# Queries, keys and values stored tile by tile, queries in half-tile buffers: a hybrid attention block on one core

## The chip, the cores and the metric

The kernel runs on one core of a Trainium2 chip. The metric is the device time of one execution in microseconds (us). A core has five engines that run side by side, each with its own in-order list of instructions: TensorE (PE, matrix products), VectorE (DVE), ScalarE (ACT), GpSimd (POOL) and SyncE (SP), which here issues every DMA. Sixteen DMA engines move data between DRAM and the on-chip memory of 128 partitions.

## The reference

One decoder block over 2048 tokens of width 1024, in float32:

```python
h = rmsnorm(x, norm1_g)
p = h @ w_in                                  # 2560 columns: pool 256, diff q/k/v 512 each, sb q/k/v 256 each
a = pool_mixer(p[pool])                       # trailing means over 2/4/8/16 tokens, 64x64 maps
b = (softmax(q1 k1') - lam * softmax(q2 k2')) v   # 4 differential heads, causal, two 64-wide maps, 128-wide values
c = A v                                       # 4 stick-breaking heads of 64, A[t,s] = sigmoid(z_ts) * prod (1 - sigmoid(z_tj))
x = x + concat(a, norm(b), norm(c)) @ w_out
x = x + (silu(h2 @ w_gate) * (h2 @ w_up)) @ w_down,  h2 = rmsnorm(x, norm2_g)
return rmsnorm(x, final_norm_g)
```

## The kernel before

The work has three parts, all of them planned together: `a1_tile` (L534) normalizes a tile of 512 tokens and projects it with the ten 256-column units of W_in; `attention` (L838) goes over the query tiles `t` = 0 to 3 and, in each, over six head pairs (four differential, two stick-breaking) in the order of `ORDER[t]`; `out_proj` (L936) and `mlp` (L963) follow. Almost every matrix product is made of three products of a high and a low part (`mm3`, L473), so queries, keys and values are stored as high and low parts too. They go to DRAM from `a1_tile` and come back in `attention`.

Nothing is issued in the order of the source. Each operation is handed to a planner (`Plan`, L102) with its engine, an estimated duration in ns, what it reads and writes, and a priority; `schedule` (L145) plays the operations against these estimates and fixes the order of every engine, and `issue` emits them in that order. All DMAs form one list, issued by SP. A buffer comes from a `Ring` (L70) of slots; a slot that two rings share passes to the second one when the first has made its last buffer. Projections of later tiles have low priority on TensorE and fill what attention leaves.

The parts that the change touches:

- DRAM layout (L301 to L304): `q_d[p]` and `k_d[p]` hold, for a pair, the high and the low part of all 2048 tokens in 128 rows (two 64-wide maps or heads); `vd_d[p]` and `vs_d[h]` hold the values.
- Stores (L586 to L613): the values of a block of 256 tokens go out per head (L595). Queries are scaled by 0.125 and split by ScalarE (L601) and VectorE (L603), keys by `split` (L414), and each goes out as one store of 512 KB (L611).
- `load_q` (L622) takes a buffer from ring `q0` for the high parts and one from `q1` for the low parts, and fills each with two loads, since the 64 rows are wanted twice, in partitions 0 to 63 and 64 to 127. Ring `q0` owns slots 31 and 12, `q1` slots 32 and 13 (L1399); 12 and 13 first belong to ring `wr` (L1386), the raw weights of `a1_tile`.
- `load_kv` (L632) loads one chunk of 512 keys: two loads for the keys (high parts in partitions 0 to 63, low parts in 64 to 127, both maps side by side), one for the values of a differential pair (L640), two for those of a stick-breaking pair (L645).
- `scores` (L651) makes the scores of 128 queries (`g` = 0 to 3 in the tile) with a chunk: the product of the keys with the high parts (L657), that with the low parts (L658), and on the diagonal the mask (L660). A differential pair goes through `g` in order with both maps of each; a stick-breaking pair goes through all four `g` for its first head and then for its second.

Of the kernel before, what the change touches and what calls it, by code (L numbers as in the profile page):

```python
# [19 lines left out]
P = 128  # L20
# [27 lines left out]
def f32(ap):  # L48
    return ap.bitcast(F32)
# [205 lines left out]
def dve_ns(n):  # L255
    return 1.042 * n + 68
# [14 lines left out]
def dma_ns(nbytes):  # L271
    return max(nbytes / 360.0, 450.0)
# [3 lines left out]
def hybrid_block_kernel(  # L276
# [21 lines left out]
    const = ctx.enter_context(tc.tile_pool(name="const", bufs=1))  # L298
    dram = ctx.enter_context(tc.tile_pool(name="dram", bufs=1, space=bass.MemoryType.DRAM))

    q_d = [dram.tile([2, P, S], F32, name=f"q_d{p}") for p in range(PAIRS)]  # L301
    k_d = [dram.tile([2, P, S], F32, name=f"k_d{p}") for p in range(PAIRS)]
    vd_d = [dram.tile([P, S // P, 2, P], F32, name=f"vd_d{p}") for p in range(DIFF_PAIRS)]
    vs_d = [dram.tile([P, S // P, 2, 64], F32, name=f"vs_d{p}") for p in range(2 * SB_PAIRS)]  # L304
    o_d = [dram.tile([KB, P, TQ], F32, name=f"o_d{t}") for t in range(NT)]
    wo_d = [dram.tile([2, P, KB, 256], F32, name=f"wo_d{u}") for u in range(4)]
    x2_d = [dram.tile([4, P, D], F32, name=f"x2_d{t}") for t in range(NT)]
# [226 lines left out]
    def a1_tile(pl, rg, t, prio, prio_pe, first):  # L534
# [8 lines left out]
            pl.op("dma", 450, lambda: nc.sync.dma_start(g1_sb, g1), w=[c_g1], prio=prio_x)  # L543
        hk = norm_transpose(pl, rg, first if t == 0 else rg["dense"], rg["hk"], xs, g1_sb, c_g1, prio_x, prio_pe, t == 0)
        if t == 0:
            constants(pl, {"w": rb["q1"], "h": rb["p0"]}, prio + 0.5, xs[3:])
        late = []
        for un in UNITS[t]:
            parts = load_split(pl, rg, w_in[un], prio, xs if t == 0 and un == UNITS[0][0] else ())
# [29 lines left out]
            for c, ps in enumerate(pend):  # L579
                if un == 0:  # L580
                    late = pend
                    break
                st = rg["st"].new()
                if is_v:
                    nh, e = (2, 128) if un != 9 else (4, 64)
                    stv = lambda st=st, nh=nh: st.t.rearrange("p a (h b l e) -> p (a h) b l e", h=nh // 2, b=2, l=2)  # L586
                    pv = lambda ps=ps, nh=nh: ps.t.rearrange("p (b h e) -> p b h e", b=2, h=nh)
                    for h in range(nh):
                        split(pl, lambda h=h, stv=stv: stv()[:, h, :, 0, :], lambda h=h, stv=stv: stv()[:, h, :, 1, :],
                              lambda h=h, pv=pv: pv()[:, :, h, :], TQ // nh, True, [ps], (st, (h, 0)), (st, (h, 1)),  # L590
                              prio)
                        dst = vs_d[h] if un == 9 else vd_d[2 * (un - 5) + h]
                        pr = DIFF_PAIRS + h // 2 if un == 9 else 2 * (un - 5) + h
                        blk0 = 4 * t + 2 * c
                        pl.op("dma", dma_ns(P * 4096 // nh), lambda dst=dst, blk0=blk0, h=h, stv=stv: nc.sync.dma_start(  # L595
                            dst[:, blk0:blk0 + 2, :, :], f32(stv()[:, h])), r=[(st, (h, 0)), (st, (h, 1))],
                            w=[(m_v[pr][t], (c, h))], prio=prio)
                else:
                    isq = un in (1, 2, 7)
                    if isq:  # L600
                        pl.op("act", act_ns(TQ), lambda st=st, ps=ps: nc.scalar.mul(st.t[:, 0, :], ps.t, 0.125),  # L601
                              r=[ps], w=[(st, 0)], prio=prio)
                        pl.op("dve", dve_ns(TQ), lambda st=st, ps=ps: nc.vector.scalar_tensor_tensor(  # L603
                            st.t[:, 1, :], ps.t, 0.125, f32(st.t[:, 0, :]), ALU.mult, ALU.subtract),
                            r=[ps, (st, 0)], w=[(st, 1)], prio=prio)
                    else:
                        split(pl, lambda st=st: st.t[:, 0, :], lambda st=st: st.t[:, 1, :], lambda ps=ps: ps.t,
                              TQ, True, [ps], (st, 0), (st, 1), prio)
                    pair = {1: 0, 2: 2, 7: 4, 3: 0, 4: 2, 8: 4}[un] + c
                    dst, mk = (q_d, m_q) if isq else (k_d, m_k)  # L610
                    pl.op("dma", dma_ns(P * 4096), lambda st=st, dst=dst[pair]: nc.sync.dma_start(  # L611
                        dst[:, :, t0:t0 + TQ].rearrange("l p t -> p l t"), f32(st.t)),
                        r=[st], w=[mk[pair][t]], prio=prio)  # L613
        for c, ps in enumerate(late):
            pool_mix(pl, rg, t, c, ps, prio, prio_pe)
        for hf, (wh, wl) in enumerate(load_split(pl, rg, w_out[t], prio)):
# [3 lines left out]


    def load_q(pl, rg, t, p, prio):  # L622
        q = [rg["q0"].new(), rg["q1"].new()]
        for hl in range(2):
            for dup in range(2):
                pl.op("dma", dma_ns(64 * 4096) * 1.3, lambda hl=hl, dup=dup: nc.sync.dma_start(
                    f32(q[hl].t[64 * dup:64 * dup + 64]),
                    q_d[p][hl, :, t * TQ:(t + 1) * TQ].rearrange("(r d) t -> d r t", r=2)),
                    r=[m_q[p][t]], w=[(q[hl], dup)], prio=prio)
        return q  # L630

    def load_kv(pl, rg, p, j, prio):  # L632
        k, v = rg["k"].new(), rg["v"].new()
        for hl in range(2):
            pl.op("dma", dma_ns(64 * 4096) * 1.3, lambda hl=hl: nc.sync.dma_start(
                f32(k.t[64 * hl:64 * hl + 64]),
                k_d[p][hl, :, j * TQ:(j + 1) * TQ].rearrange("(r d) t -> d r t", r=2)),
                r=[m_k[p][j]], w=[(k, hl)], prio=prio)
        if p < DIFF_PAIRS:
            pl.op("dma", dma_ns(P * 4096), lambda: nc.sync.dma_start(  # L640
                f32(v.t), vd_d[p][:, 4 * j:4 * j + 4].rearrange("p b l e -> p (b l e)")),
                r=[m_v[p][j]], w=[v], prio=prio)
        else:
            for r in range(2):
                pl.op("dma", dma_ns(P * 2048), lambda r=r: nc.sync.dma_start(  # L645
                    f32(v.t[:, r * TQ:(r + 1) * TQ]),
                    vs_d[2 * (p - DIFF_PAIRS) + r][:, 4 * j:4 * j + 4].rearrange("p b l e -> p (b l e)")),
                    r=[m_v[p][j]], w=[(v, r)], prio=prio)
        return k, v

    def scores(pl, rg, q, kt, r, g, j, t, strict, prio):  # L651
        n = TQ if j < t else (g + 1) * P
        s = rg["s"].new()
        qs = slice(g * P, (g + 1) * P)

        def qk():
            nc.tensor.matmul(s.t[:, :n], q[0].t[:, r, qs], kt.t[:, r, :n], start=True, stop=False)  # L657
            nc.tensor.matmul(s.t[:, :n], q[1].t[:, r, qs], kt.t[:, r, :n], start=False, stop=j < t)  # L658
            if j == t:
                nc.tensor.matmul(s.t[:, n - P:n], identb, masks[:, strict, :], start=False, stop=True)  # L660

        pl.op("pe", 2 * mm_ns(n) + (60 if j == t else 0), qk, r=[*q, kt], w=[s], prio=prio)
        return s, n

    def weighted(pl, rg, rows, nkp, pv, q0, vmm, v_bufs, nmm, prio):
# [710 lines left out]
    def banks(ids):  # L1376
# [19 lines left out]
    )  # L1396
    rb.update(
        k=ring([2, TQ], F32R, ("w", R(23, 27)), ("w", R(0, 2))), v=ring([D], F32R, ("w", R(27, 31)), ("w", R(2, 4))),
        q0=ring([2, TQ], F32R, ("w", [31, 12])), q1=ring([2, TQ], F32R, ("w", [32, 13])),  # L1399
        p0=ring([TQ], F32, ("h", R(7, 15)), ("w", [20, 21])), p1=ring([TQ], F32, ("h", R(15, 20))),  # L1400
        th=ring([TQ], F32R, ("h", [20, 21, 22, 4])), tl=ring([TQ], F32R, ("h", [23, 24, 25, 5])),
        w=ring([TQ], F32, ("h", R(26, 28))), iv=ring([TQ + 1], F32, ("h", R(28, 30))),
# [70 lines left out]
```

## Time and profile before

| | |
|---|---|
| median of 3 runs | 2723.2 us (2714.47 to 2727.28) |
| profiled execution, its own time | 2719.03 us |
| its span | 2717.2 us |
| mean granted TensorE clock | 0.977 of full speed |
| busy: TensorE, VectorE, ScalarE, GpSimd | 96%, 66%, 49%, 32% |
| DMA, mean rate | 167 GB/s, 454.27 MB |

The profile shows one execution. "PE L657 <- DMA d<-q_d" reads: TensorE's instruction of line 657 waited for a transfer from `q_d` into an on-chip buffer (all of those are called `d`). PEld is the loading of the stationary matrix, which overlaps PE; SPq is SP's list of DMA issues. A granted clock of 1.00 is 2.4 GHz; the other level is 1.2 GHz, and a stretch shows the mean. The attention part runs from about 137 us, overlapped by projections until some 900 us and by the output projection after that.

### The profile page before, as it was taken

The numbers are of one execution on the slowest core, as the hardware profiler recorded it, in microseconds if no ns is written. First come the engines' busy times: TensorE is split into PE (matmuls) and PEld (weight loads), VectorE is DVE, ScalarE is ACT, GpSimd is POOL, SyncE is SP. The second block draws the span as 40 slices with busy tenths as digits, with TensorE's granted clock in tenths as the row PEclk, the third lists the DMA queues.
The fourth block names the chain that finished last, engine by engine and source line by source line (L and its number), as shares of the span: only waits on it lengthen the run. The fifth ranks groups of instructions, "written<-read, shape, count | busy, mean of one in ns | idle before, by whom it ended". The sixth has DMA issues, their size and how long they took to land.

```text
span 2717.2 us, 39503 instructions
## 1 busy us (share of the span) xinstructions
PE 2601.9 (96%) x13836; PEld 2176.7 (80%) x13836; DVE 1786.2 (66%) x3131; ACT 1319.3 (49%) x2645; POOL 870.0 (32%) x890
## 2 busy tenths in 40 slices
PE   9989989989999999999989999999999998999998
PEld 7878778877888788888978877888888886888886
DVE  6366787758887888788656666545444447558557
ACT  4365566646666666665534444323333333445444
POOL 1001212212254124133015456535454544132041
PEclk9989999989999999999999999999999999999999
DMA  6786585556564775664534457465222338335223
GB/s 217 245 251 184 160 245 160 155 155 202 153 177 147 225 203 147 192 178 161 166 118 155 155 184 239 158 220 199 101 102 97 109 129 291 118 95 194 93 90 120
DMA packets 223480, 454.27 MB, mean 167 GB/s; under 512 B 23720, under 2 KB 70952, under 8 KB 223280
## 3 DMA queue, kind: packets, MB, share of 16 engines
q1 hardware_dynamic: 223280, 451.75, 52.9%
q8 instruction: 108, 1.77, 0.3%
q14 instruction: 92, 0.75, 0.1%
HBM read 321.11 MB, written 130.55 MB: 166 GB/s over the span
## 4 chain that ended last, share of the span: by engine, by line
PE 72%; DMA 9%; DVE 9%; issue 3%; ACT 2%; POOL 1%; SPq 1%; DVEq 0%; ACTq 0%; POOLq 0%
PE bank L474 16%; PE bank L476 16%; PE bank L475 16%; DVE d L416 4%; DMA d<-q_d 4%; PE bank L657 3%; PE bank L681 3%; PE bank L658 3%; DMA d<-wo_d 2%; PE bank L924 2%; PE bank L923 2%; PE bank L925 2%; ACT d L415 1%; PE bank L562 1%; PE bank L781 1%
## 5 line engine op out<-in xcount | busy, mean ns | idle before, releaser
L474 PE MATMUL bank<-d 128*128 128x512 f32 x2296 | 919.0, 400 | 14.0 <-DVE d L1122 9.8
L476 PE MATMUL bank<-d 128*128 128x512 f32 x2296 | 910.3, 396 | 5.7 <-DVE d L416 5.4
L416 DVE TENSOR_TENSOR d<-d 128x512 fp32r<-128x512 f32 (+2 forms) x672 | 614.6, 938 | 457.5 <-ACT d L415 281.2
L475 PE MATMUL bank<-d 128*128 128x512 f32 x2296 | 909.3, 396 | 3.4 <-DVE d L416 3.4
L415 ACT CAST d<-d 128x512 fp32r<-128x512 f32 (+2 forms) x672 | 489.0, 758 | 651.0 <-PE bank L476 352.3
L961 POOL TENSOR_TENSOR d<-d 128x512 f32<-128x512 f32 x336 | 520.0, 1556 | 846.3 <-DVE d L416 622.9
L474 PEld LDWEIGHTS bank<-d 128*128 128x128 f32 x2296 | 435.7, 190 | 116.0 <-DVE d L1122 12.4
L476 PEld LDWEIGHTS bank<-d 128*128 128x128 f32 x2296 | 434.3, 189 | 110.3 <-DVE d L416 8.7
L475 PEld LDWEIGHTS bank<-d 128*128 128x128 f32 x2296 | 434.8, 189 | 101.3 <-DVE d L416 5.1
L416 DVE TENSOR_TENSOR d<-bank,d 128x512 fp32r<-128x512 f32 (+3 forms) x381 | 219.3, 603 | 139.7 <-ACT d L415 138.7
L819 POOL TENSOR_TENSOR d<-d 128x512 f32<-128x512 f32 (+3 forms) x160 | 160.4, 1003 | 397.9 <-DVE d L815 375.6
L415 ACT CAST d<-bank 128x512 fp32r<-128x512 f32 (+3 forms) x381 | 187.5, 529 | 194.0 <-PE bank L681 122.0
L729 ACT ACTIVATE d<-bank,d 128x512 f32<-128x512 f32 (+3 forms) x320 | 198.9, 627 | 128.4 <-DVE d L726 120.3
L751 POOL TENSOR_SCALAR d<-d 128x512 f32<-128x512 f32 (+3 forms) x144 | 95.8, 681 | 448.7 <-ACT d L741 318.1
L726 DVE TENSOR_REDUCE d<-bank 128x1 f32<-128x512 f32 (+3 forms) x320 | 186.9, 602 | 61.6 <-PE bank L658 31.1
L657 PE MATMUL bank<-d 128*128 128x512 f32 (+3 forms) x480 | 203.7, 425 | 24.8 <-ACT d L729 9.0
L658 PE MATMUL bank<-d 128*128 128x512 f32 (+3 forms) x480 | 181.9, 382 | 25.5 <-DMA d<-q_d 25.5
L1122 DVE TENSOR_TENSOR d<-bank,d 128x512 f32<-128x512 f32 x176 | 121.0, 687 | 116.0 <-PE bank L476 98.7
L815 DVE TENSOR_TENSOR_SCAN d<-d,bank 128x512 f32<-128x512 f32 (+3 forms) x160 | 174.3, 1090 | 19.6 <-ACT d L807 8.1
L1118 ACT COPY d<-bank 128x512 f32<-128x512 f32 x132 | 77.3, 586 | 221.7 <-PE bank L476 196.9
L681 PE MATMUL bank<-ident,d 128*128 128x128 f32 x1088 | 157.5, 279 | 3.4 <-DVE d L772 2.6
L923 PE MATMUL bank<-d 128*128 128x256 f32 x512 | 149.5, 292 | 2.8 <-DMA d<-wo_d 1.1
(133 smaller groups left out, 3593.5 us busy)
## 6 DMA issues: line engine op xcount, KB each, us to landing
d<-in_w_gu_dram SPq DMA_DIRECT2D x88, 512.0 KB, 3.5
d<-in_w_in_dram SPq DMA_DIRECT2D x80, 512.0 KB, 4.6
d<-k_d SPq DMA_DIRECT2D x120, 256.0 KB, 6.6
d<-wo_d SPq DMA_DIRECT2D x52, 512.0 KB, 6.0
d<-q_d SPq DMA_DIRECT2D x96, 256.0 KB, 6.3
d<-vd_d SPq DMA_DIRECT2D x40, 512.0 KB, 4.9
g_d<-d SPq DMA_DIRECT2D x66, 256.0 KB, 2.1
d<-g_d SPq DMA_DIRECT2D x66, 256.0 KB, 2.7
```

Source lines behind the costliest of these rows:

```text
L415: pl.op("act", act_ns(n, psum), lambda: nc.scalar.copy(hi(), src()), r=r, w=[whi], prio=prio)
L416: pl.op("dve", dve_ns(n), lambda: nc.vector.tensor_sub(lo(), src(), f32(hi())), r=[*r, *after, whi], w=[wlo], prio=prio)
L474: nc.tensor.matmul(o, a_hi, b_hi, start=first, stop=False, **kw)
L475: nc.tensor.matmul(o, a_hi, b_lo, start=False, stop=False, **kw)
L476: nc.tensor.matmul(o, a_lo, b_hi, start=False, stop=last, **kw)
L657: nc.tensor.matmul(s.t[:, :n], q[0].t[:, r, qs], kt.t[:, r, :n], start=True, stop=False)
L658: nc.tensor.matmul(s.t[:, :n], q[1].t[:, r, qs], kt.t[:, r, :n], start=False, stop=j < t)
L681: nc.tensor.transpose(tp.t[:, c:c + P], rows[qb][kb // 4].t[:, (kb % 4) * P:(kb % 4 + 1) * P], ident)
L726: pl.op("dve", dve_ns(n), lambda s=s, n=n, mc=mc, sm=sm: nc.vector.tensor_reduce(sm.t[:, mc:mc + 1], s.t[:, :n], AX, ALU.max, negate=True) ...
L729: pl.op("act", act_ns(n, True, 2), lambda s=s, n=n, e=e, mc=mc, lc=lc, sm=sm: nc.scalar.activation(e.t[:, :n], s.t[:, :n], AF.Exp, bias=sm ...
L923: nc.tensor.matmul(o, m[:, 0, cs], wh.t[:, k % 4, :], start=k == 0, stop=False)
L961: pl.op(eng, ns, lambda: en.tensor_tensor(out(), a(), b(), op), r=r, w=w, prio=prio)
```

## The change

- In DRAM, each pair and token tile has an array of its own: `q_d[p][t]` is [2 halves of 256 queries, 64 rows, 2 maps, 2 parts (high, low), 256 queries], `k_d[p][t]` is [2 parts, 64 rows, 2 maps, 512 keys], `v_d[p][t]` is 128 rows of 1024 values.
- A query or key store becomes two stores of 64 partitions each, one for a map (or head); the query buffer that is stored now has its columns ordered half, part, query. A value store has the same size as before.
- `load_q` takes two buffers from one ring `q` with the four slots 31, 32, 12 and 13. A buffer holds one half of the tile's queries, both maps, high and low parts, and is filled by one load whose source is read twice (`to_broadcast`, leading dimension 2), for partitions 0 to 63 and 64 to 127.
- A key chunk and a value chunk are one load of 512 KB each.
- `scores` reads the buffer of its half only, and depends on that alone.
- The constants of the head take their scratch buffer from ring `q` instead of `q1`.

```diff
@@ -298,10 +298,10 @@
     const = ctx.enter_context(tc.tile_pool(name="const", bufs=1))
     dram = ctx.enter_context(tc.tile_pool(name="dram", bufs=1, space=bass.MemoryType.DRAM))
 
-    q_d = [dram.tile([2, P, S], F32, name=f"q_d{p}") for p in range(PAIRS)]
-    k_d = [dram.tile([2, P, S], F32, name=f"k_d{p}") for p in range(PAIRS)]
-    vd_d = [dram.tile([P, S // P, 2, P], F32, name=f"vd_d{p}") for p in range(DIFF_PAIRS)]
-    vs_d = [dram.tile([P, S // P, 2, 64], F32, name=f"vs_d{p}") for p in range(2 * SB_PAIRS)]
+
+    q_d = [[dram.tile([2, 64, 2, 2, 256], F32, name=f"q_d{p}_{t}") for t in range(NT)] for p in range(PAIRS)]
+    k_d = [[dram.tile([2, 64, 2, TQ], F32, name=f"k_d{p}_{t}") for t in range(NT)] for p in range(PAIRS)]
+    v_d = [[dram.tile([P, D], F32, name=f"v_d{p}_{t}") for t in range(NT)] for p in range(PAIRS)]
     o_d = [dram.tile([KB, P, TQ], F32, name=f"o_d{t}") for t in range(NT)]
     wo_d = [dram.tile([2, P, KB, 256], F32, name=f"wo_d{u}") for u in range(4)]
     x2_d = [dram.tile([4, P, D], F32, name=f"x2_d{t}") for t in range(NT)]
@@ -543,7 +543,7 @@
             pl.op("dma", 450, lambda: nc.sync.dma_start(g1_sb, g1), w=[c_g1], prio=prio_x)
         hk = norm_transpose(pl, rg, first if t == 0 else rg["dense"], rg["hk"], xs, g1_sb, c_g1, prio_x, prio_pe, t == 0)
         if t == 0:
-            constants(pl, {"w": rb["q1"], "h": rb["p0"]}, prio + 0.5, xs[3:])
+            constants(pl, {"w": rb["q"], "h": rb["p0"]}, prio + 0.5, xs[3:])
         late = []
         for un in UNITS[t]:
             parts = load_split(pl, rg, w_in[un], prio, xs if t == 0 and un == UNITS[0][0] else ())
@@ -589,28 +589,30 @@
                         split(pl, lambda h=h, stv=stv: stv()[:, h, :, 0, :], lambda h=h, stv=stv: stv()[:, h, :, 1, :],
                               lambda h=h, pv=pv: pv()[:, :, h, :], TQ // nh, True, [ps], (st, (h, 0)), (st, (h, 1)),
                               prio)
-                        dst = vs_d[h] if un == 9 else vd_d[2 * (un - 5) + h]
                         pr = DIFF_PAIRS + h // 2 if un == 9 else 2 * (un - 5) + h
-                        blk0 = 4 * t + 2 * c
-                        pl.op("dma", dma_ns(P * 4096 // nh), lambda dst=dst, blk0=blk0, h=h, stv=stv: nc.sync.dma_start(
-                            dst[:, blk0:blk0 + 2, :, :], f32(stv()[:, h])), r=[(st, (h, 0)), (st, (h, 1))],
-                            w=[(m_v[pr][t], (c, h))], prio=prio)
+                        o0, w = (h % 2 * TQ if un == 9 else 0) + 4 * c * e, 4 * e
+                        pl.op("dma", dma_ns(P * 4096 // nh), lambda dst=v_d[pr][t], o0=o0, w=w, h=h, stv=stv: nc.sync.dma_start(
+                            dst[:, o0:o0 + w], f32(stv()[:, h].rearrange("p b l e -> p (b l e)"))),
+                            r=[(st, (h, 0)), (st, (h, 1))], w=[(m_v[pr][t], (c, h))], prio=prio)
                 else:
                     isq = un in (1, 2, 7)
                     if isq:
-                        pl.op("act", act_ns(TQ), lambda st=st, ps=ps: nc.scalar.mul(st.t[:, 0, :], ps.t, 0.125),
+                        part = lambda l, st=st: st.t.rearrange("p h (l t) -> p h l t", l=2)[:, :, l, :]
+                        src = lambda ps=ps: ps.t.rearrange("p (h t) -> p h t", h=2)
+                        pl.op("act", act_ns(TQ), lambda part=part, src=src: nc.scalar.mul(part(0), src(), 0.125),
                               r=[ps], w=[(st, 0)], prio=prio)
-                        pl.op("dve", dve_ns(TQ), lambda st=st, ps=ps: nc.vector.scalar_tensor_tensor(
-                            st.t[:, 1, :], ps.t, 0.125, f32(st.t[:, 0, :]), ALU.mult, ALU.subtract),
+                        pl.op("dve", dve_ns(TQ), lambda part=part, src=src: nc.vector.scalar_tensor_tensor(
+                            part(1), src(), 0.125, f32(part(0)), ALU.mult, ALU.subtract),
                             r=[ps, (st, 0)], w=[(st, 1)], prio=prio)
                     else:
                         split(pl, lambda st=st: st.t[:, 0, :], lambda st=st: st.t[:, 1, :], lambda ps=ps: ps.t,
                               TQ, True, [ps], (st, 0), (st, 1), prio)
                     pair = {1: 0, 2: 2, 7: 4, 3: 0, 4: 2, 8: 4}[un] + c
                     dst, mk = (q_d, m_q) if isq else (k_d, m_k)
-                    pl.op("dma", dma_ns(P * 4096), lambda st=st, dst=dst[pair]: nc.sync.dma_start(
-                        dst[:, :, t0:t0 + TQ].rearrange("l p t -> p l t"), f32(st.t)),
-                        r=[st], w=[mk[pair][t]], prio=prio)
+                    for r in range(2):
+                        pl.op("dma", dma_ns(P * 2048), lambda st=st, dst=dst[pair][t], r=r, isq=isq: nc.sync.dma_start(
+                            dst[:, :, r].rearrange("h d l t -> d h (l t)" if isq else "l d t -> d l t"),
+                            f32(st.t[64 * r:64 * r + 64])), r=[st], w=[(mk[pair][t], r)], prio=prio)
         for c, ps in enumerate(late):
             pool_mix(pl, rg, t, c, ps, prio, prio_pe)
         for hf, (wh, wl) in enumerate(load_split(pl, rg, w_out[t], prio)):
@@ -620,46 +622,35 @@
 
 
     def load_q(pl, rg, t, p, prio):
-        q = [rg["q0"].new(), rg["q1"].new()]
-        for hl in range(2):
-            for dup in range(2):
-                pl.op("dma", dma_ns(64 * 4096) * 1.3, lambda hl=hl, dup=dup: nc.sync.dma_start(
-                    f32(q[hl].t[64 * dup:64 * dup + 64]),
-                    q_d[p][hl, :, t * TQ:(t + 1) * TQ].rearrange("(r d) t -> d r t", r=2)),
-                    r=[m_q[p][t]], w=[(q[hl], dup)], prio=prio)
+
+        q = []
+        for h in range(2):
+            qh = rg["q"].new()
+            q.append(qh)
+            pl.op("dma", dma_ns(P * 4096), lambda h=h, qh=qh: nc.sync.dma_start(
+                f32(qh.t), q_d[p][t][h].rearrange("(o d) r l t -> o d (r l t)", o=1).to_broadcast([2, 64, D])),
+                r=[m_q[p][t]], w=[qh], prio=prio)
         return q
 
     def load_kv(pl, rg, p, j, prio):
         k, v = rg["k"].new(), rg["v"].new()
-        for hl in range(2):
-            pl.op("dma", dma_ns(64 * 4096) * 1.3, lambda hl=hl: nc.sync.dma_start(
-                f32(k.t[64 * hl:64 * hl + 64]),
-                k_d[p][hl, :, j * TQ:(j + 1) * TQ].rearrange("(r d) t -> d r t", r=2)),
-                r=[m_k[p][j]], w=[(k, hl)], prio=prio)
-        if p < DIFF_PAIRS:
-            pl.op("dma", dma_ns(P * 4096), lambda: nc.sync.dma_start(
-                f32(v.t), vd_d[p][:, 4 * j:4 * j + 4].rearrange("p b l e -> p (b l e)")),
-                r=[m_v[p][j]], w=[v], prio=prio)
-        else:
-            for r in range(2):
-                pl.op("dma", dma_ns(P * 2048), lambda r=r: nc.sync.dma_start(
-                    f32(v.t[:, r * TQ:(r + 1) * TQ]),
-                    vs_d[2 * (p - DIFF_PAIRS) + r][:, 4 * j:4 * j + 4].rearrange("p b l e -> p (b l e)")),
-                    r=[m_v[p][j]], w=[(v, r)], prio=prio)
+        pl.op("dma", dma_ns(P * 4096), lambda: nc.sync.dma_start(
+            f32(k.t), k_d[p][j].rearrange("l d r t -> (l d) r t")), r=[m_k[p][j]], w=[k], prio=prio)
+        pl.op("dma", dma_ns(P * 4096), lambda: nc.sync.dma_start(f32(v.t), v_d[p][j]), r=[m_v[p][j]], w=[v], prio=prio)
         return k, v
 
     def scores(pl, rg, q, kt, r, g, j, t, strict, prio):
         n = TQ if j < t else (g + 1) * P
         s = rg["s"].new()
-        qs = slice(g * P, (g + 1) * P)
+        qh, c0 = q[g // 2], 2 * r * 256 + g % 2 * P
 
         def qk():
-            nc.tensor.matmul(s.t[:, :n], q[0].t[:, r, qs], kt.t[:, r, :n], start=True, stop=False)
-            nc.tensor.matmul(s.t[:, :n], q[1].t[:, r, qs], kt.t[:, r, :n], start=False, stop=j < t)
+            nc.tensor.matmul(s.t[:, :n], qh.t[:, c0:c0 + P], kt.t[:, r, :n], start=True, stop=False)
+            nc.tensor.matmul(s.t[:, :n], qh.t[:, c0 + 256:c0 + 256 + P], kt.t[:, r, :n], start=False, stop=j < t)
             if j == t:
                 nc.tensor.matmul(s.t[:, n - P:n], identb, masks[:, strict, :], start=False, stop=True)
 
-        pl.op("pe", 2 * mm_ns(n) + (60 if j == t else 0), qk, r=[*q, kt], w=[s], prio=prio)
+        pl.op("pe", 2 * mm_ns(n) + (60 if j == t else 0), qk, r=[qh, kt], w=[s], prio=prio)
         return s, n
 
     def weighted(pl, rg, rows, nkp, pv, q0, vmm, v_bufs, nmm, prio):
@@ -1396,7 +1387,7 @@
     )
     rb.update(
         k=ring([2, TQ], F32R, ("w", R(23, 27)), ("w", R(0, 2))), v=ring([D], F32R, ("w", R(27, 31)), ("w", R(2, 4))),
-        q0=ring([2, TQ], F32R, ("w", [31, 12])), q1=ring([2, TQ], F32R, ("w", [32, 13])),
+        q=ring([D], F32R, ("w", [31, 32, 12, 13])),
         p0=ring([TQ], F32, ("h", R(7, 15)), ("w", [20, 21])), p1=ring([TQ], F32, ("h", R(15, 20))),
         th=ring([TQ], F32R, ("h", [20, 21, 22, 4])), tl=ring([TQ], F32R, ("h", [23, 24, 25, 5])),
         w=ring([TQ], F32, ("h", R(26, 28))), iv=ring([TQ + 1], F32, ("h", R(28, 30))),
```

## Rows read from the trace of the kernel before

**Rows 1.** The page: the span, and busy time of each engine.

```profile
span 2717.2 us, 39503 instructions
PE 2601.9 (96%) x13836; PEld 2176.7 (80%) x13836; DVE 1786.2 (66%) x3131; ACT 1319.3 (49%) x2645; POOL 870.0 (32%) x890
```

**Rows 2.** The page: the chain that ended last, shares of the span by line.

```profile
PE bank L474 16%; PE bank L476 16%; PE bank L475 16%; DVE d L416 4%; DMA d<-q_d 4%; PE bank L657 3%; PE bank L681 3%; PE bank L658 3%; DMA d<-wo_d 2%; PE bank L924 2%; PE bank L923 2%; PE bank L925 2%; ACT d L415 1%; PE bank L562 1%; PE bank L781 1%
```

**Rows 3.** The chain in order of time: start us, us, what; query loads alone.

```profile
173.27 5.71 DMA d<-q_d
...
878.08 7.62 DMA d<-q_d
```

**Rows 4.** Waits of TensorE, 137 to 1200 us: us in total, times, longest us.

```profile
PE bank L658 <- DMA d<-q_d: 25.5, 14, 3.7
...
PE bank L657 <- DMA d<-k_d: 6.5, 3, 3.4
...
PE bank L657 <- DMA d<-q_d: 2.0, 3, 1.3
```

**Rows 5.** Timeline, 378 to 402 us: start us, us, engine, line, op, tiles, count, [idle before].

```profile
379.09 0.40 PE L658 MATMUL bank<-d 128*128 128x512 f32 x1
379.28 2.54 SPq L626 DMA_DIRECT2D d<-q_d  x4
...
387.61 0.19 PEld L658 LDWEIGHTS bank<-d 128*128 128x128 f32 x1 [1.25 <-DMA d<-q_d]
```

**Rows 6.** L657 alone by stretch: PE and PEld busy us (count), clock, DMA share, GB/s.

```profile
137.00:264.00 127.00, 18.53 (x48) 9.83 (x47) 0.93 0.73 215
...
884.00:1300.00 416.00, 83.02 (x192) 37.19 (x192) 0.97 0.62 182
```

**Rows 7.** All instructions, same stretches: busy PE, PEld, DVE, ACT, POOL, clock, DMA share, GB/s.

```profile
137.00:264.00 127.00, 115.93 (x789) 102.65 (x789) 87.82 (x202) 77.13 (x183) 14.41 (x31) 0.93 0.73 215
264.00:518.00 254.00, 235.48 (x1418) 202.74 (x1416) 192.52 (x396) 157.82 (x366) 64.49 (x108) 0.95 0.64 183
518.00:884.00 366.00, 340.96 (x1993) 289.40 (x1993) 274.16 (x494) 221.92 (x506) 112.08 (x166) 0.96 0.57 167
884.00:1300.00 416.00, 400.48 (x2740) 353.23 (x2741) 345.76 (x631) 263.16 (x612) 115.83 (x191) 0.97 0.62 182
```

**Rows 8.** DMA issues: tiles, op, count, KB each, median us from issue to landing.

```profile
d<-k_d SPq DMA_DIRECT2D x120, 256.0 KB, 6.6
...
d<-q_d SPq DMA_DIRECT2D x96, 256.0 KB, 6.3
d<-vd_d SPq DMA_DIRECT2D x40, 512.0 KB, 4.9
...
q_d<-d SPq DMA_DIRECT2D x24, 512.0 KB, 3.4
...
d<-vs_d SPq DMA_DIRECT2D x40, 256.0 KB, 4.1
...
d<-in_hsel_dram SPq DMA_DIRECT2D x1, 24.0 KB
```

**Rows 9.** Rate of the DMA engines: two stretches as in rows 7; the page's queue line.

```profile
4.00:7.00 3.00, 3.00 (x12) 1.24 (x11) 1.14 (x8) 2.30 (x4) 0.00 (x0) 1.00 0.99 393
1800.00:1850.00 50.00, 50.00 (x218) 40.54 (x217) 22.74 (x23) 15.86 (x22) 24.38 (x18) 1.00 0.95 342
q1 hardware_dynamic: 223280, 451.75, 52.9%
```

**Rows 10.** Timeline of SP around a pair boundary in tile 2.

```profile
690.93 2.96 SPq L626 DMA_DIRECT2D d<-q_d  x4
...
697.62 1.88 SPq L635 DMA_DIRECT2D d<-k_d  x3
```

**Rows 11.** SP's issues by line: count, ns min/median/max, first and last start us.

```profile
L626 SPq DMA_DIRECT2D d<-q_d x96: 573/580/1285, 38.3 to 1149.7; - x96
L611 SPq DMA_DIRECT2D q_d<-d x24: 370/374/547, 29.9 to 869.4; - x24
```

## The prediction

> **What bounds the kernel now.** I read the page first: TensorE is busy for 2601.9 us of a span of 2717.2 us [rows 1], so time is to be won or lost only where TensorE waits or where something else sets its pace. Next I read the chain of work that ended last: query loads hold 4% of it, about 100 us, the largest share of any transfer [rows 2]. In order of time these are 14 long pieces, from 173 to 878 us, of 5.7 to 8.6 us each, of which the first and the last stand here [rows 3]. A chain share is not a prize: while such a load was under way TensorE did projections that the planner had put there. What it really stood still for is in the view of waits: 25.5 us in 14 waits ahead of L658 and 2.0 us in 3 ahead of L657, together 27.5 us; key loads cost 6.5 us more [rows 4]. The timeline of one boundary between two head pairs shows why: the last score of a pair is made at 379.1 us, the four query loads of the next pair are issued at 379.3 us, as the buffer comes free, and the second product of the new pair stands until 387.6 us [rows 5]. Attention is thus single-buffered in its queries until W_in's buffers (slots 12, 13) come free. Last I cut the span where the query tiles begin: the four stretches hold 48 scores in the first to 192 in the last, 8 for each pair and chunk [rows 6], and in these TensorE's granted clock is 0.93 to 0.97, and the DMA engines are busy for 0.57 to 0.73 of the time [rows 7].
>
> **The change part by part**, against the profiled execution's own 2719.0 us (span 2717.2 and 1.8 around it); the median of the runs shown, 2723.2, is 4.2 us above it.
>
> *Buffers.* Today a pair needs two buffers until its last score; after the change each buffer holds one query half, high and low parts together, and is free when that half's scores are done. With two slots, the first half of the next pair is loaded while the second half's scores run. For differential pairs that is half a pair ahead; for a stick-breaking pair, where each half is used again for the second head, about a quarter. In tile 1 a pair lasts 254/6 = 42 us [rows 7], so 10 to 20 us stand against a landing of 6.3 us [rows 8]. If the new load lands as the old one did, all 27.5 us go: **-27.5 us**. Next late would be the key chunk.
>
> *The query load itself.* Four transfers of 256 KB become two of 512 KB, and the bytes remain the same. But the source is now a pattern whose leading dimension counts 2 (a stride of zero, to write both copies at once), where each of today's loads leads with 64 rows. The trace of before has no such load, so I bound it. From below: a 512 KB value load with 4 KB rows, 4.9 us to landing [rows 8]. From above: only as many engines carry it as the leading dimension counts, two, with 256 KB each. An engine moves 393/(0.99 x 16) = 24.8 GB/s in a stretch of wide input rows, 342/(0.95 x 16) = 22.5 in one of weight loads, and 451.75 MB/(0.529 x 16 x 2717 us) = 19.6 over the whole run [rows 9]: 10.6, 11.7 or 13.4 us a load. The nearest row is that of hsel, the one group with a leading count under 16 (8 rows): it alone, of all, has no landing time [rows 8], although its data were used. Its landing signals do not add up as those of a 64- or 128-row load do. That is a hint, not a rate, but it points to fewer engines, and I take **two engines, 11 us a load**, keeping both ends.
>
> The Trainium skill states this as a rule (DMA: Bandwidth & Descriptors, section Rules for kernel authors): an outermost dimension under 16, such as a leading broadcast without stride, confines the whole transfer to at most that many engines. By that rule the sum goes as I forecast; by the 4.9 us row alone it would be the first rival below. The hsel row agrees with it, and no run here shows its rate.
>
> What two slow engines do: every later transfer also has a sixteenth of its bytes on these two, behind the queries in one queue (SP issues all), and lands only when that part has landed. Their work by tile, from the busy shares [rows 7]:
> Tile 0, 127 us: 0.73 x 127 = 92.7 us, less 24 old loads of 16 KB an engine at 215/(0.73 x 16) = 18.4 GB/s, 21.4 us, plus 6 pairs x 2 x 11 = 132: 203 us. **+76 us**.
> Tile 1, 254 us: 162.6 - 22.0 + 132 = 273 us. **+18 us**.
> Tile 2, 366 us: 208.6 - 21.5 + 132 = 319 us, 87% full. Tile 3 with the output projection, 416 us: 257.9 - 17.9 (20 loads) + 5 x 22 = 350 us, 84%.
> In the last two the work fits, but each pair's keys can stand behind a query half: at 690.9 us the query loads go out, and three key transfers follow them at 697.6 us [rows 10]. A key load then lands up to 11 us later than now, at the price of nothing if TensorE has other work in its order and of 11 if not; I take the middle, 5.5 us for 12 pairs: **+66 us**.
>
> *Clock.* The first three tiles lost 0.07 x 127 + 0.05 x 254 + 0.04 x 366 = 36 us of clock beside 127 + 254 + 366 - 115.9 - 235.5 - 341.0 = 55 us of idle [rows 7], 0.66 us for one. About 132 us more idle could cost 87 more. I take nothing, as the stalls grow longer rather than more numerous; 87 is kept as an upper end.
>
> *Stores.* 48 stores of 512 KB become 96 of 64 partitions: 48 x 0.37 = 18 us more of SP's time; the loads save 48 + 60 + 20 issues at 0.58 us, 74 us [rows 8, 11]. SP waits for data most of the time, so neither is on the path; if SP became the limit, the net would be a gain. Runs in DRAM stay 2 KB (1 KB for stick-breaking values), so a store's landing stays near its 3.4 us [rows 8]; the store stands ahead of its reader by tens of us, except for a pair that is used as soon as its unit is done.
>
> *Keys and values.* Key loads go from two halves in 2 KB runs to 4 KB rows, stick-breaking values from two to one. At 24.8 instead of 18.4 GB/s a chunk's 32 KB an engine take 1.3 instead of 1.8 us; that is 3 to 6 us in tiles 0 and 1, taken as nothing, and with the 6.5 us of key waits a lower end of -12.
>
> *Scaling and new order.* ScalarE's and VectorE's query splits keep their element counts; only the views differ: nothing, since neither engine bounds the stage. A score now needs one half alone, so the planner lays out another order. It plans a query load at 1.5 us plus lags and knows nothing of engines; 30 us either way, about the size of the 27.5 us of waits its present error allows.
>
> Sum: 2719.0 - 27.5 + 76 + 18 + 66 = 2851.5; with 4.2 for the median, **2856 us**.
>
> **The rivals.** *Sixteen engines after all* (faster). The load lands in about 5 us, well inside half a pair; 27.5 us go, and a third of the 36 us of clock, 12: 2723 - 39 = 2684, or 2696 without the clock. For it: equal bytes, wide rows. Against it: the leading 2 and the hsel row. It decides from the point where a load's landing is below the time between a half's last score and the next pair's first, some 10 us in tile 0 (six pairs in 127 us make 21 a pair).
> *A key wait takes the place* (no change). Queries are early on sixteen engines, but the key chunk, issued when the last scores free its buffer [rows 10] and landing in 6.6 us [rows 8] against 6.3 for the queries, now holds the pair's start; 27.5 us come back as key waits: 2723. Against it: today's key waits are only 6.5 us [rows 4], and the first chunk of tiles 0 to 2 has a spare slot.
> *Two engines, but only the queries late.* If what follows is not held up, tile 0 alone pays, six pairs at about 5 us beyond the gap: 2723 - 27.5 + 30 = 2726 at the least; each bit of hold-up then moves it toward the forecast. I count this as the low edge of the forecast case.
>
> **How the numbers follow.** Two engines 0.82, sixteen engines and faster 0.12, key waits in place 0.06. About 0.5%, 14 us, is what a measurement of this kernel tells from no change; the forecast case lies beyond that but for its low edge. Its low end: 10.6 us a load, no hold-up in tiles 2 and 3, -12 for keys, -30 for order: 2719 - 27.5 + 71 + 13 - 12 - 30 + 4 = 2738. Its high end: 13.4 us a load (105 + 47 in tiles 0 and 1), 12 x 13.4 = 161, and 87 of clock: 3096. The range is cut where this case thins out, 2740 to 3070; it leaves out the rivals and little else.
>
> **What would show it.** Query loads, 48 of 512 KB, without a landing time, as hsel has none; key, value and W_in loads landing some 5 to 15 us later than now; TensorE's waits for DMA in the attention tiles above 100 us where 34 stand now; tile 0 stretched to some 200 us at fewer GB/s; a lower granted clock there. The forecast is wrong if query loads land in 5 us, or if tile 0 keeps its 127 us.

## The result and the profile after

The changed kernel takes 2919.8 us in the median (2915.9 to 2922.2), the kernel before 2722.3 (four runs now): a ratio of 1.0727 (95% interval 1.0697 to 1.0756). The forecast was 2856 us, in a range of 2740 to 3070. The profiled execution took 2915.9 us.

The page after, its lines on the span and the engines, the granted clock and the DMA engines (compare [rows 1]):

```profile
span 2914.1 us, 39424 instructions
PE 2626.5 (90%) x13836; PEld 2200.2 (76%) x13836; DVE 1791.1 (61%) x3131; ACT 1330.8 (46%) x2649; POOL 873.7 (30%) x890
...
PEclk8977899899999998989899999999999999999999
DMA  5753455444554445445354445646433227534433
...
DMA packets 205143, 454.26 MB, mean 156 GB/s; under 512 B 21768, under 2 KB 69000, under 8 KB 204944
```

TensorE does the same 13,836 products and stands still for 2914.1 - 2626.5 = 288 us instead of 115. The bytes are the same; the sixteen DMA engines are less busy on average, and yet TensorE waits longer for what they carry.

The same stretches as in [rows 7], cut again where a tile's first score is made; the last line is all that follows attention:

```profile
150.00:338.00 188.00, 121.33 (x718) 108.12 (x716) 81.91 (x193) 73.92 (x176) 14.80 (x31) 0.77 0.41 133
338.00:628.00 290.00, 235.09 (x1409) 201.73 (x1409) 192.72 (x395) 156.57 (x362) 65.88 (x108) 0.92 0.50 160
628.00:1009.00 381.00, 332.97 (x1990) 286.04 (x1991) 273.06 (x493) 229.19 (x510) 111.67 (x163) 0.95 0.50 158
1009.00:1450.00 441.00, 390.42 (x2523) 337.15 (x2522) 334.53 (x597) 255.35 (x591) 114.97 (x188) 0.91 0.49 161
1450.00:2914.00 1464.00, 1414.30 (x6498) 1156.90 (x6497) 843.12 (x1303) 564.08 (x930) 553.76 (x375) 0.99 0.45 151
```

Tile 0 takes 188 us where it took 127, at 133 GB/s instead of 215, and its granted clock falls from 0.93 to 0.77 of full speed, a mix of the two levels of 2.4 and 1.2 GHz. Who TensorE waits for, first lines of its waits over the whole run (compare [rows 4]):

```profile
PE bank L648 <- DMA d<-q_d: 90.7, 18, 8.7
PE bank L648 <- DMA d<-k_d: 29.5, 3, 13.4
PE bank L882 <- DVE d L887: 21.7, 3, 15.4
PE bank L914 <- DMA d<-wo_d: 16.7, 3, 15.1
```

The DMA issues (compare [rows 8]):

```profile
d<-in_w_gu_dram SPq DMA_DIRECT2D x88, 512.0 KB
d<-in_w_in_dram SPq DMA_DIRECT2D x80, 512.0 KB
d<-v_d SPq DMA_DIRECT2D x60, 512.0 KB
d<-k_d SPq DMA_DIRECT2D x60, 512.0 KB
...
d<-q_d SPq DMA_DIRECT2D x48, 512.0 KB
```

No group has a landing time any more, not only the queries: with 48 loads that signal their end fewer than sixteen times, the view's pairing of issues and landings seems to fit for none. How many times they signal can be read from the packets, since each signal is a small one. The kernel before had 23720 packets under 512 B:

```profile
DMA packets 223480, 454.27 MB, mean 167 GB/s; under 512 B 23720, under 2 KB 70952, under 8 KB 223280
```

Queries, keys and values need 80 issues fewer now (48 + 60 + 20 loads less, 48 stores more). At sixteen signals each that makes 1280 small packets fewer; 23720 - 21768 = 1952 are gone. (The first experiment below bears the sixteen out: it has 32 issues fewer than the kernel before, and 23208 small packets, 512 = 32 x 16 fewer.) The other 672 are 48 x 14: **each query load has two signals instead of sixteen**. The Trainium skill says so (DMA: Bandwidth & Descriptors, section Why a DMA increments its semaphore by 16 and not by 1): only the engines that a transfer uses signal its end, and their number is the largest up to sixteen that divides the leading counts of both sides. Here the counts are 2 and 128, and the trace agrees.

The rate of a slow load shows where little else is under way. Four stretches of the changed kernel, columns as in [rows 7]:

```profile
163.00:170.00 7.00, 0.66 (x4) 0.42 (x4) 4.29 (x6) 3.51 (x8) 0.00 (x0) 0.71 0.13 52
187.00:193.00 6.00, 5.61 (x24) 5.02 (x25) 1.81 (x3) 1.26 (x2) 0.00 (x0) 0.50 0.13 52
193.00:196.00 3.00, 3.00 (x24) 2.69 (x24) 1.15 (x5) 3.00 (x8) 0.00 (x0) 0.97 0.13 51
516.00:525.00 9.00, 0.00 (x0) 0.00 (x0) 0.08 (x1) 0.59 (x1) 0.00 (x0) 0.50 0.13 51
```

A share of 0.13 of sixteen engines is what two full ones make, and 51 to 52 GB/s between them is some 26 GB/s for one. At that rate the 512 KB of a load take 10.1 to 10.3 us. Cut into stretches of 1 us, tile 0 has 83 of 188 at such a share (0.12 to 0.14), and 9 in which next to nothing moves (under 0.03). The first two stretches lie at two waits of TensorE, each shown by the instruction that ends it:

```profile
172.13 0.45 PE L648 MATMUL bank<-d 128*128 128x128 f32 x1 [7.13 <-DMA d<-q_d]
...
187.39 0.66 PE L648 MATMUL bank<-d 128*128 128x384 f32 x1 [8.32 <-DMA d<-q_d]
```

### The profile page after: what moved, and what is told of

Same layout as the page of the kernel before. It is cut to its first block, busy times and chain, and to the rows that moved or that the text cites. A ratio compares the mean times of both kernels' runs of the same rounds, so it can differ in the third digit from the quotient of the medians.

```text
span 2914.1 us, 39424 instructions
## 1 busy us (share of the span) xinstructions
PE 2626.5 (90%) x13836; PEld 2200.2 (76%) x13836; DVE 1791.1 (61%) x3131; ACT 1330.8 (46%) x2649; POOL 873.7 (30%) x890
## 2 busy tenths in 40 slices
DMA packets 205143, 454.26 MB, mean 156 GB/s; under 512 B 21768, under 2 KB 69000, under 8 KB 204944
## 5 line engine op out<-in xcount | busy, mean ns | idle before, releaser
L474 PEld LDWEIGHTS bank<-d 128*128 128x128 f32 x2296 | 435.3, 190 | 119.5 <-DVE d L1113 13.7
L476 PEld LDWEIGHTS bank<-d 128*128 128x128 f32 x2296 | 433.9, 189 | 107.5 <-DVE d L416 7.3
L475 PEld LDWEIGHTS bank<-d 128*128 128x128 f32 x2296 | 434.6, 189 | 99.8 <-DVE d L416 4.8
L648 PE MATMUL bank<-d 128*128 128x512 f32 (+3 forms) x480 | 208.7, 435 | 159.8 <-DMA d<-q_d 90.7
L416 DVE TENSOR_TENSOR d<-bank,d 128x512 fp32r<-128x512 f32 (+4 forms) x381 | 220.4, 605 | 167.0 <-ACT d L415 157.9
L415 ACT CAST d<-bank 128x512 fp32r<-128x512 f32 (+4 forms) x381 | 188.2, 527 | 257.0 <-PE bank L672 169.0
L648 PEld LDWEIGHTS bank<-d 128*128 128x128 f32 x480 | 98.2, 205 | 197.4 <-issue 100.0
L649 PE MATMUL bank<-d 128*128 128x512 f32 (+3 forms) x480 | 184.2, 387 | 0.0
```

What stands on the lines that cost most here:

```text
L415: pl.op("act", act_ns(n, psum), lambda: nc.scalar.copy(hi(), src()), r=r, w=[whi], prio=prio)
L416: pl.op("dve", dve_ns(n), lambda: nc.vector.tensor_sub(lo(), src(), f32(hi())), r=[*r, *after, whi], w=[wlo], prio=prio)
L474: nc.tensor.matmul(o, a_hi, b_hi, start=first, stop=False, **kw)
L475: nc.tensor.matmul(o, a_hi, b_lo, start=False, stop=False, **kw)
L476: nc.tensor.matmul(o, a_lo, b_hi, start=False, stop=last, **kw)
L648: nc.tensor.matmul(s.t[:, :n], qh.t[:, c0:c0 + P], kt.t[:, r, :n], start=True, stop=False)
```

## The experiments

The code below is cut to the call or the argument that differs.

**The load alone undone.** Plan, layout and buffers stay as changed; the body of the one operation issues two loads.

```diff
-nc.sync.dma_start(f32(qh.t), q_d[p][t][h].rearrange("(o d) r l t -> o d (r l t)", o=1).to_broadcast([2, 64, D]))
+for dup in range(2):
+    nc.sync.dma_start(f32(qh.t[64 * dup:64 * dup + 64]), q_d[p][t][h].rearrange("d r l t -> d (r l t)"))
```

> The changed kernel with its plan, its layout and its buffers untouched; only each query half is filled by two loads of 64 partitions, each leading with 64 rows, instead of one whose source leads with 2. Theory (the leading 2 puts a query load on two DMA engines): the load lands in about 6 us, TensorE's 90.7 us of waits ahead of L648 for queries nearly vanish, tile 0 goes back to 125-135 us, and the half-tile buffers now show their worth: 2680 to 2710 us, below the kernel before. Rival (the new order or layout is at fault, the loads only show it): still over 2850. Between the two, 2720 to 2850, both have a part.

Measured: 2691.1 us, 0.9881 of the kernel before (0.9854 to 0.9908). The tiles of this run, its issue line for the queries, and its waits for them:

```profile
138.00:246.00 108.00, 96.85 (x719) 85.81 (x717) 79.64 (x190) 72.82 (x176) 14.76 (x31) 0.98 0.77 226
246.00:488.00 242.00, 228.72 (x1407) 194.45 (x1408) 187.98 (x395) 154.11 (x359) 64.24 (x102) 0.98 0.63 194
488.00:828.00 340.00, 324.55 (x1991) 278.42 (x1990) 273.23 (x495) 228.60 (x512) 113.10 (x166) 0.99 0.58 177
828.00:1222.00 394.00, 380.82 (x2526) 329.65 (x2525) 336.60 (x601) 257.12 (x595) 118.38 (x193) 0.97 0.57 180
```

```profile
d<-q_d SPq DMA_DIRECT2D x96, 256.0 KB, 4.5
```

```profile
PE bank L651 <- DMA d<-q_d: 3.4, 2, 2.4
```

So 229 us hang on the shape of 48 loads, and the rest of the change gains 31 us against 2722.3. Tile 0 falls below the 127 us of before, to 108, where 125 to 135 had been expected. None of these 108, cut into stretches of 1 us, has a share of 0.12 to 0.14.

**The load alone done, in the kernel before.** Its four loads of 256 KB stay four; each now writes both copies.

```diff
-f32(q[hl].t[64 * dup:64 * dup + 64]), q_d[p][hl, :, t * TQ:(t + 1) * TQ].rearrange("(r d) t -> d r t", r=2)
+f32(q[hl].t[:, r, :]), q_d[p][hl, 64 * r:64 * r + 64, t * TQ:(t + 1) * TQ].rearrange("(o d) t -> o d t", o=1).to_broadcast([2, 64, TQ])
```

> The kernel before with its plan, layout, buffers and count and size of loads untouched; each of the four query loads of a pair now writes both copies of one map's high or low part, from a source that leads with 2 and 64 rows behind it, in 2 KB runs. Theory: two engines carry 128 KB each of every load, 6.5 us at 20 GB/s, 26 us for the four against some 8 now; in tiles 0 to 2 nothing hides them, 17 pairs x 18 us = 306 us: about 3000 us (2900 to 3100). Rival (order or layout at fault): 2720 as before.

Measured: 3067.1 us, 1.1267 of the kernel before (1.1231 to 1.1303), inside the range of the theory. The page's packets:

```profile
DMA packets 222136, 454.27 MB, mean 148 GB/s; under 512 B 22376, under 2 KB 69608, under 8 KB 221936
```

The issues are as many as before, and 23720 - 22376 = 1344 = 96 x 14 signals are missing. Neither layout nor order is needed for the loss. It is larger than that of the change, perhaps since the half-tile buffers, which fetch queries earlier, are missing; no run separates that from the other layout and the smaller loads.

**Only the first halves slow.** In the run with two loads, the load that leads with 2 is kept where `h == 0`.

> As the run with two loads for each half, but the first half of each pair keeps its single load that leads with 2: half the work on the two engines, same plan. If the price is full engines (203 us of work in tile 0's 127, 273 in tile 1's 254), half of it nearly fits (137 and 207 us): at most 40 us above the run with two loads. If each slow load has its own price, about half of the distance between the two kernels, 110 us above it.

Measured: 2832.3 us, 141 above the run with two loads: more than half of the 229 for half of the slow loads. My expectation for full engines fell. Its sum was also made on the wrong base: without slow loads tile 0 needs 108 us, not 127. With half of them it took 159 us:

```profile
143.00:302.00 159.00, 107.27 (x719) 96.77 (x717) 81.02 (x193) 73.27 (x176) 14.76 (x31) 0.83 0.54 163
```

That is 20 us above an estimate of what two engines have to do there: 0.77 x 108 = 83 us, less some 10 for the queries now moved differently, plus 66, makes 139. And 141 - (159 - 108) = 90 us arise outside tile 0, where by the same kind of estimate the engines have room.

**Only tiles 0 and 1 slow** (the load that leads with 2 is kept where `t < 2`).

> As the run with two loads for each half, but query tiles 0 and 1 keep the load that leads with 2. The prediction's sum gives these tiles 76 + 18 of 160 us: 94 us above the run with two loads, 70 to 140. If the hold-up of tiles 2 and 3 is what costs, under 50.

Measured: 2832.6 us, 141 above the run with two loads, just over the upper end of 140. By difference, tiles 2 and 3 then hold 2919.8 - 2832.6 = 87 us.

**Only the second halves slow** (where `h == 1`).

> As the run with two loads for each half, but now the second half of each pair alone keeps its single load that leads with 2 (the run before had the first halves, 2832 us against 2691). If a slow load costs what it comes too late for its own scores, second halves cost less than first halves, since their buffer comes free at the end of the pair before and the first half's scores lie between: 2710 to 2770. If the price is the load on the two engines, whichever half it is: 2820 to 2845.

Measured: 2813.3 us, 122 above: just under the second expectation's range, far above the first's. First halves cost 19 us more than second halves, so coming too late for its own scores has a part in a slow load's price, but a small one. A slow load costs 122/24 = 5.1 to 141/24 = 5.9 us when half of them are slow and 229/48 = 4.8 when all are.

**Another list.** The query loads of the changed kernel go out from ScalarE (`nc.scalar.dma_start`); then the same with two loads.

> The changed kernel; its query loads, still one for each half and leading with 2, are issued by ScalarE instead of SP, so that other transfers are not in the same list behind them. If the price is the hold-up of the other transfers behind the queries on two engines: 2720 to 2790. If it is the queries' own lateness: 2850 or more. ScalarE then also waits where SP waited; the next run shows what that alone costs.

> The run with two loads of 64 partitions for each half (2691 us), these loads issued by ScalarE. It shows what ScalarE pays for issuing 96 loads of some 0.6 us and for waiting in its own order: 0 to 40 us above 2691. It is the base that the run before is to be read against.

Measured: 2942.9 us, and 2705.0 with two loads: the slow loads cost 238 us here too. Taking the queries out of SP's list helps nothing, so standing behind them in one list is not the price by itself.

**The two engines loaded by somebody else.** In the run with two loads a transfer that nobody reads follows each half; in the second version it is spread. `idle_d[n]` is a DRAM array of its own for each half, [2, 65, D + 16] and [P, D + 16], so that its rows don't run together.

```diff
+nc.sync.dma_start(idle_d[n][:, :64, :D], x[0:P, :].rearrange("(o d) c -> o d c", o=2))
```
```diff
+nc.sync.dma_start(idle_d[n][:, :D], x[0:P, :])
```

> The run with two loads for each half (2691 us), and behind each half an added transfer of 512 KB in 4 KB rows from DRAM to DRAM that nobody reads, whose destination leads with 2. The queries keep their sixteen engines; the two engines get the changed kernel's extra work. If the hold-up of all transfers on the two engines is the price: 2800 to 2950. If it is the queries' own lateness: under 2730.

> The same added transfers, but leading with 128 rows, so on sixteen engines: what their bytes alone cost, without the two full engines. 24 MB more at some 200 GB/s, beside other work: 2691 to 2720 us. The distance from the run before is the price of two engines.

Measured: 2923.8 us when it leads with 2, and 2708.7 when spread. **The queries are on sixteen engines here, and yet 2923.8 - 2691.1 = 233 us are lost, where the changed kernel loses 229.** The added bytes themselves cost 18 us when spread, so 215 us belong to the two engines. The packets show the engines: of small ones there are 23304 - 23208 = 96 = 48 x 2 more than with two loads alone, and 23976 - 23208 = 768 = 48 x 16 more when spread.

```profile
DMA packets 212824, 479.44 MB, mean 164 GB/s; under 512 B 23304, under 2 KB 70536, under 8 KB 212624
```
```profile
DMA packets 213496, 479.44 MB, mean 177 GB/s; under 512 B 23976, under 2 KB 71208, under 8 KB 213296
```

TensorE's waits with the two engines loaded show that keys, and queries too, now come late without being slow loads themselves:

```profile
PE bank L653 <- DMA d<-k_d: 55.4, 6, 17.6
PE bank L653 <- DMA d<-q_d: 49.6, 10, 9.3
...
PE bank L919 <- DMA d<-wo_d: 15.7, 1, 15.7
```

**The planner told of the lateness.** The changed kernel, with 12 us added to the time at which the planner takes a query load's data to be ready.

> The changed kernel; the planner alone is told that a query load's data are ready 12 us later than it reckons, so that it orders TensorE's other work ahead of the scores. If the price is the queries' own lateness against an order that expects them early, most of it goes: 2720 to 2800. If the two engines and what stands behind the queries on them set the pace, the order helps little: 2880 to 2930.

Measured: 2884.3 us, 36 below the changed kernel and inside the second expectation, at its lower edge. Waits move rather than go: 41.5 us for queries, 54.9 for keys.

```profile
PE bank L649 <- DMA d<-k_d: 54.9, 7, 15.9
PE bank L649 <- DMA d<-q_d: 41.5, 11, 8.4
```

This order hides part of the lateness of the queries (90.7 us of waits in the changed kernel), but more of the lateness of the keys now shows (29.5 there). Key loads have sixteen signals, and so a share on the two engines too. One value, 12 us, was tried, and for the queries alone.

**Which part of the change gains.** In the run with two loads the planner holds both halves to the pair's last score.

```diff
-r=[qh, kt], w=[s]
+r=[*q, kt], w=[s]
```

> The run with two loads for each half (2691 us), but the planner is told that every score reads both halves, so both buffers are held to the pair's last score, as before the change. If the half-tile buffers bring the 34 us below the kernel before: 2715 to 2735. If it is the layout and the whole key and value chunks: 2691 to 2700.

Measured: 2708.9 us, 0.995 of the kernel before (0.9926 to 0.9974), between the two expectations: of the gain about 18 us belong to the half-tile buffers, and some 13 (7 to 20 by the interval) to layout and whole chunks. Waits for queries are 12.4 us here, 3.4 with the halves and 27.5 before.

**One load, other order of dimensions.** Query row d goes to partitions 2d and 2d + 1, and the keys' high and low rows are laid to match (`k_d` is [64, 2 parts, 2, TQ] then).

```diff
-q_d[p][t][h].rearrange("(o d) r l t -> o d (r l t)", o=1).to_broadcast([2, 64, D])
+q_d[p][t][h].rearrange("(d o) r l t -> d o (r l t)", o=1).to_broadcast([64, 2, D])
-k_d[p][j].rearrange("l d r t -> (l d) r t")
+k_d[p][j].rearrange("d l r t -> (d l) r t")
```

> The changed kernel with one load for each half still, but the copies side by side: query row d goes to partitions 2d and 2d + 1, so the source leads with 64 rows and the broadcast of 2 comes second; key rows are stored so that the high and the low part of a row lie in partitions 2d and 2d + 1 too, and the products sum over the same pairs in another order. If the leading dimension alone decides, all transfers have sixteen engines again, and with 48 issues fewer than with two loads a half: 2675 to 2700 us, no trace of the 229. If any broadcast is slow, wherever its dimension stands: over 2850.

Measured: 2691.3 us, 0.9871 of the kernel before (0.9848 to 0.9895). The load of 512 KB now lands in 4.6 us, and TensorE hardly waits for it; issues, packets and waits:

```profile
d<-k_d SPq DMA_DIRECT2D x60, 512.0 KB, 4.9
...
d<-q_d SPq DMA_DIRECT2D x48, 512.0 KB, 4.6
```

```profile
DMA packets 205815, 454.26 MB, mean 169 GB/s; under 512 B 22440, under 2 KB 69672, under 8 KB 205616
```

```profile
PE bank L648 <- DMA d<-q_d: 0.3, 1, 0.3
```

Small packets: 23720 - 22440 = 1280 = 80 x 16, none missing. A broadcast is not slow; its place in the pattern was. It ties with the run with two loads, so 48 issues fewer buy nothing here, and both beat the kernel before.

## Why the prediction was right, and where it was off

- *Two engines, 11 us a load.* Right: two signals a load, two engines busy where the slow loads are alone, and 10.1 to 10.3 us for 512 KB at the rate measured there. The loss goes with the leading dimension alone, in both kernels and for a transfer that nobody reads. The rival with sixteen engines (2684 to 2696 us) is what one gets with the dimensions in the other order, 2691.3. Tile 0 fits: 203 us of work were forecast from 137 us on, and the next tile's first score is made at 338 us, 201 us later. That it is so close is partly luck, since the tile itself began late, at 150 us, and took 188. Of the other signs, TensorE's waits ahead of L648 for queries and keys are 90.7 + 29.5 = 120 us, above the 100 named, and the clock fell. The missing landing times tell less than was thought: every group lacks them, so neither late queries nor late others can be read from them.
- *-27.5 us for waits.* With the loads repaired the gain is 31 us. The buffers, which were to bring all of it, bring 18; 13 come from layout and whole chunks, which had been taken as nothing with a lower end of -12. That the sum is near 27.5 is luck in part.
- *Tiles 0 and 1, +94 us.* By the run with these alone slow, 141. *Tiles 2 and 3, +66 us.* By difference, 87. Both are low, and by the clocks of the four tiles (0.77, 0.92, 0.95 and 0.91, with two loads 0.97 to 0.99) both contain the next term.
- *Clock, nothing.* This is the mis-sized term: it holds 43 of the 69 us by which the price of the slow loads came out above the forecast (229 for 160). Against the run with two loads, TensorE stands still for 179 us more (288 against 2691.7 - 2583.3 = 108) and is busy for 2626.5 - 2583.3 = 43 us more with the same products. 160 us of waits and 0 of clock were forecast. In tile 0 the same products (718 and 719 in the records) take 121.3 instead of 96.9 us, at a granted clock of 0.77 instead of 0.98. "The stalls grow longer rather than more numerous" was no reason, as the stretches in the section on the result show: a wait of 8.3 us for queries ends at 187.4 us, and TensorE then works until 193 us at 0.50, the level of 1.2 GHz, before it is back at 0.97.
- *Fullness as the mechanism.* Only partly right. In tile 0 next to nothing moves in 9 of 188 stretches of 1 us, in tile 1 in 22 of 290, so tile 0 and, less so, tile 1 are full by what can be seen. But half the slow loads cost more than half, and 87 us arise, by difference, in tiles whose engines have room by the prediction's own sum (87% and 84%). There a pair costs 87/12 = 7.3 us, where the hold-up was taken as 5.5. What in these tiles is hold-up and what is clock was not measured apart.
- *Stores, SP.* A store of 64 partitions takes SP 0.60 us instead of the 0.37 reckoned. Stores were said to stand well ahead of their readers, except for a pair that is used at once; in the changed kernel one such store is late. In the timeline, in tile 1, the key store goes out at 507.6 us, the key loads that wait for it at 524.6 us, and TensorE waits until 528.0 us; from 516 to 525 us only two engines are busy (the last of the four stretches above). SP's own wait for such stores, here from 137 to 700 us, is 11.9 us at the longest, with two loads 4.8 in the whole run:

```profile
495.02 0.54 SPq L630 DMA_DIRECT2D d<-q_d  x1
496.10 7.62 SPq L639 DMA_DIRECT2D d<-v_d  x1
...
507.59 3.25 SPq L613 DMA_DIRECT2D k_d<-d  x2
...
524.55 1.27 SPq L637 DMA_DIRECT2D d<-k_d  x3
```

```profile
527.96 0.45 PE L648 MATMUL bank<-d 128*128 128x128 f32 x1 [13.39 <-DMA d<-k_d]
```

```profile
SPq L637 <- DMA k_d<-d: 18.6, 4, 11.9
```

What stays open: why the price is the same when ScalarE issues the queries. The queries have two engines there too (21768 small packets, as in the changed kernel). How an engine shares its time between two lists, no view shows; that run fits both a hold-up of the others and a longer landing of the queries themselves (its waits for queries are 122.7 us, for keys 24.4).

## What to carry to other kernels

Read the leading dimension of both sides of a transfer before its size: here a broadcast of 2 in front cost 229 us, and behind a dimension of 64 nothing that could be measured. If the on-chip order stands in the way, let the rows of the other operand move, as in the last experiment. A transfer on few engines is not priced by its own landing alone: 215 us were lost here to transfers that nobody read. Count the work of the fullest engine, not the mean busy share. And when waits grow, price the clock too: here 43 us came with 179 of idle time.

## What had not been expected of the hardware

SP itself gets stuck while it issues. The value load above took 7.62 us to issue. By line, the count and the shortest, median and longest issue in ns, first of value and key loads, then of query stores, in the changed kernel:

```profile
L639 SPq DMA_DIRECT2D d<-v_d x60: 314/323/7617, 75.9 to 1380.2; - x60
```

```profile
L637 SPq DMA_DIRECT2D d<-k_d x60: 319/354/5958, 101.8 to 1359.0; - x60
```

```profile
L613 SPq DMA_DIRECT2D q_d<-d x48: 574/600/7584, 30.0 to 1037.0; - x48
```

Before, the longest query store took 547 ns [rows 11]. The stretch from 163 to 170 us above, in which only two engines are busy, holds such an issue, of a load of W_in that has sixteen engines:

```profile
163.65 6.01 SPq L412 DMA_DIRECT2D d<-in_w_in_dram  x1
```

An issue that lasts so long suggests that the list of a full engine takes no more until something has left it; no run was made to show that. The loss does not need it, though. When ScalarE issues the queries, nothing sticks, neither SP's issues (the longest of all takes 1.65 us) nor ScalarE's, and the slow loads cost 238 us all the same:

```profile
L639 SPq DMA_DIRECT2D d<-v_d x60: 319/320/710, 72.1 to 1406.9; - x60
```

```profile
L630 ACTq DMA_DIRECT2D d<-q_d x48: 488/490/1084, 39.3 to 1340.4; - x48
```
